# A one-core decoder layer: four places for v tiles on their way out, squares behind the splits, and gate rows turned by TensorE

## Chip, cores and metric

The kernel runs on one core of a Trainium2 chip. The metric is the device time of one execution in microseconds (us), the median over runs. All arithmetic is float32: each operand of a product is split into a rounded high part and a low remainder, and every product is made of three TensorE passes (high by high, high by low, low by high).

## The reference, cut to what matters

```
mod = silu(c) @ w_ada + b_ada;  shift, scale, gate = split(mod, 3)
h = rmsnorm(x, g) * (1 + scale) + shift                      # x is 512 tokens by 2048
q_lat, kv_lat, k_rope, z_mla, u, v, z_sgu, g_mla, g_sgu = split(h @ w_in)
A = causal attention from q_lat, kv_lat, k_rope (16 heads), times silu(z_mla)
v = rmsnorm(v, sgu_norm_g)                                   # a norm over all 2048 columns of v
B = u * (tril(W_s) v_chunk + b_s), times silu(z_sgu)         # 16 groups of 128 columns
merged = sigmoid(g_mla) * A + sigmoid(g_sgu) * B
x = x + gate * (merged @ w_out);  return rmsnorm(x, final_norm_g)
```

Three things of it matter here. The norm of v needs the sum of squares over all columns of v, so the pieces of v are squared as they are made (`ssv`), written out to a DRAM scratch tensor (`v_d`), and read back by group after the norm is known. The gate is a vector over 2048 columns; it is computed with the columns on the partitions (`gate`, 128 by 16), and is needed along the free dimension for all partitions (`grow`). So it goes through a DRAM scratch tensor, `gate_row` (16 by 128), and comes back as a broadcast. And `sigmoid(g_mla) * silu(z_mla)` of head 14 is built from a z that was made early and stored (`z_d`).

## The kernel before, in words

The kernel streams all weights once. A weight granule (128 by up to 1024 numbers) is loaded by SyncE's queue (SP) into one of a few raw places, split by ScalarE (ACT, the high part: a cast) and VectorE (DVE, the low part: a subtraction) into one of two or three places for split weights, and used by TensorE (PE). The program is one list in order for each engine: nothing is reordered at run time, so an instruction that waits holds back everything behind it on its engine. SP is held in the same way: a load waits there until its raw place is free, and stores behind it wait too.

The stages around the change:

**Projection steps, `st` 0 to 25** (`for st, (cg, i) in enumerate(steps)`, L580). Columns of v in three groups `cg` of 384, 384 and 320 columns, eight steps each, and two steps for z. `get` splits the next granule, issues loads, and then runs one, two or three of the pending functions in `pend` (the number is `run`). After a group's last step four `evac_v` (L524), one for each block of 128 tokens, come due: each squares a PSUM bank into a tile (`ssv` gets the sum), copies the bank over it, and hands it to `store`. All of them, and `evac_z`, take their tile from the two places `sig`; `stores` issues a store at the end of the step after the one that made it. Two places for split weights (`w0`, `w1`) alternate, so that the split for the next step can start when the step before has ended.

**v steps, V to -1** (28 of them, V = -28; L1364 and on). The first 1024 columns of v, by seven products in place of eight (sums and differences of blocks). Twelve products a step. `early` and `on(step, phase, ...)` hold what else is done in a step; the phases run in the order FIRST, EVAC, GATE, SPLIT, BACK, then the products, then MISC and LOAD. `v_split` for step s+2 is in phase SPLIT of step s. `v_c12`, `v_c22`, `v_c11`, `v_c21` (L893 to L914) join the pieces of v; `v_done` squares a piece on ScalarE and puts its store into the next step. They run in EVAC, ahead of SPLIT, of the steps V+18, V+20, V+27 and 0.

**Slots 0 and on** (`for s, (p, k) in enumerate(order)`). 24 products of 256 columns each for two of the five other projections; again the split for slot s+2 is in phase SPLIT of slot s, with three places for split weights (`w0`, `w2`, `w1` in turn). `place` puts small VectorE work into slots with room. In slots 0 to 2 stand the end of v and the gate of head 14: `gate_op("z", 14, ..., 0)` (a sigmoid in slot 0, its product in slot 1), `v_norm` in slot 1 (the reduction of `ssv`, a square root on ScalarE, a reciprocal), and `gate_out(0, 4)` in slot 2. The first use of the norm, `sgu_scale`, is in slot 4. `v_load` reads a group of v for it.

```
on(0, EVAC, v_c21, 0)
on(1, EVAC, v_norm)
on(2, LOAD, gate_out, 0, NG)
```

`gate_out` writes four columns of `gate` straight to four rows of `gate_row`: each partition gives four single numbers, `DMA.dma_start(gate_row[a:b].rearrange("j p -> p j"), gate[:, a:b])`.

**Output steps** (L1731 and on). `out_granule(cg, i, ...)` is one granule of 1024 numbers a row of `w_out`, 24 products of 512 columns; step `8*cg + i - 3` runs from 0 (cg 0, i 3) to 20 (cg 2, i 7), and then the last group `cg` 3 runs block by block from weights kept split. In group 2 each step splits two granules, one of group 2 and one of group 3 (`dh`, `dl`), of which the weights stay. In the same steps the last twelve chunks of `w_ada` (1 MB each) are loaded and multiplied with `cact` (`chunk_sum`, twelve sums in the steps 2 to 14); after each fourth chunk (in the steps 5, 10 and 14) `gate_out` follows one step later and `grow_load` two steps later. `residual` (DVE, ACT) multiplies a finished bank with `grow` and adds x, one in each of the first four steps after a group.

Of the kernel before, what the change touches and what calls it, by code (L numbers as in the profile page):

```python
# [11 lines left out]
F32 = mybir.dt.float32  # L12
# [3 lines left out]
AF = mybir.ActivationFunctionType  # L16
# [4 lines left out]
P = 128  # L21
D = 2048
S = 512
# [6 lines left out]
GW = 1024  # L30
# [11 lines left out]
NG = 4  # L42
# [78 lines left out]
def trunk_layer(ctx, tc, xT, xn, c, vecs, pos, wada, w1, w2, wv, wv3, wv4, wh, wh15, wq, wqr, wk, wvv, wo, wsT, bsp, gfin, out,  # L121
                dbg=None):
    nc = tc.nc
    ACT, DVE, PE, DMA = nc.scalar, nc.vector, nc.tensor, nc.sync
# [36 lines left out]
    def nt(p, shape, dt, tag, **kw):  # L161
        uid[0] += 1
        return p.tile(shape, dt, tag=tag, name=f"{tag}_{uid[0]}", **kw)
# [10 lines left out]
    latp = Scope("lat", side=RIGHT)  # L174
# [112 lines left out]
    def get(i, ahead=1, run=1):  # L287
        r = ws.get(i, ahead)
        fs, pend[:] = pend[:run], pend[run:]
        for f in fs:  # L290
            f()
        return r
# [8 lines left out]
    def bank_at(k):  # L301
        return nt(psp.p, [P, S], F32, f"ps{k}")

    def bank():
        n_bank[0] += 1
        return bank_at(ring[(n_bank[0] - 1) % len(ring)])
# [217 lines left out]
    def evac_v(n, cg, ps):  # L524
        m = VW[cg] // P
        w, c0 = m * P, VC[cg]
        t = nt(tb.p, [P, S], F32, "sig", bufs=2)
        ACT.activation(t[:, :w], ps[:, :w], AF.Square, accum_out=ssv[:, n, cg:cg + 1])
        ACT.copy(t[:, :VW[cg]], ps[:, :VW[cg]])
        store(v_d[n][:, c0:c0 + w], t[:, :w])  # L530
        if cg == 2:
            store(kr_d[n], t[:, w:VW[cg]])
# [45 lines left out]
    assert (n_bank[0] - 1) % 8 == 3  # L578
    psv = {}
    for st, (cg, i) in enumerate(steps):  # L580
        wH, wL = get(gb[st], ahead=0 if st == len(steps) - 1 else 1, run={0: 3, 9: 2, 10: 2}.get(st, 1))
        if KC + st < len(DOTS):
            fix_to(FIXED[KC + st], lambda: dot_to(DOTS[KC + st]))
        if cg == "z":
            for k in range(8):
                j = 8 * i + k
                sl = slice(k * P, (k + 1) * P)
                mm3(plain, wH[:, sl], wL[:, sl], hh[j], hl[j], j == 0, j == KC - 1)
            if i == 1:
                pend.append(evac_z)  # L590
        else:
            w = VW[cg]
            if i == 0:
                psv[cg] = [bank_at(k)[:, :w] for k in v_banks[cg]]
            for k in range(2):
                j = 2 * i + k
                sl = slice(k * w, (k + 1) * w)
                for n in range(NB):
                    tk = slice(n * P, (n + 1) * P)
                    mm3(psv[cg][n], hh[j][:, tk], hl[j][:, tk], wH[:, sl], wL[:, sl], j == 0, j == KC - 1)  # L600
            if i == 7:
                for n in range(NB):
                    pend.append(lambda n=n, cg=cg, ps=psv[cg][n]: evac_v(n, cg, ps))
        if 7 <= st < 7 + NG:
            ada_dot(2 * KC + st - 7)
        if st == 8:
            xp.close()
            s12 = Scope("s12")
            for n in ("s1h", "s1l", "s2h", "s2l"):
                sums[n] = nt(s12.p, [P, 8, 256], F32R, n)  # L610
            tb = Scope("tB")
        if st == 6 + NG:
            ada.close()
            c1[0] = Scope("c1", side=RIGHT)
            for n in ("s4h", "s4l"):
                sums[n] = nt(c1[0].p, [P, 8, 256], F32R, n)
        for f in early.pop(st, ()):
            f()
        stores()
# [3 lines left out]
        cols = slice(a, b)  # L623
        tt(gate[:, cols], dots[:, 2 * KC + a:2 * KC + b], vec[:, C_BADA + 2 * KC + a:C_BADA + 2 * KC + b], ALU.add)

    def gate_out(a, b):
        DMA.dma_start(gate_row[a:b].rearrange("j p -> p j"), gate[:, a:b])

    def v_norm():
        gate_sum(0, NG)  # L630
# [9 lines left out]
    def slot(name, dt=F32):  # L640
        return nt(latp.p, [P, S], dt, name)
# [3 lines left out]
    def sig():  # L645
        n_sig[0] += 1
        return slot(f"lat{4 + n_sig[0] % 2}")
# [4 lines left out]
    def on(s, phase, f, *a):  # L652
        assert s >= done[0], (s, done)
        events.setdefault(s, {}).setdefault(phase, []).append(lambda: f(*a))
# [140 lines left out]
    def finish(k, which, s):  # L795

        ty, h = PAIRS[k]["ab".index(which)]
        gate_op(ty, h, res[k, which], s)
# [28 lines left out]
    def evacuate(p, k, s):  # L827

        ps = bank_for(p, k)
        if p == 1:  # L830
            res[k, "a"] = slot(f"lat{k % 2}")
            ACT.copy(res[k, "a"][:, left], ps)
        elif p == 6:
            res[k, "b"] = slot(f"lat{2 + k % 2}")
            ACT.copy(res[k, "b"][:, right], ps)
        elif p == 2:
            ACT.copy(res[k, "b"][:, left], ps)
        elif p == 5:
            t = res[k, "a"][:, left]
            tt(t, ps, t, ALU.add)  # L840
        elif p == 3:
            t = res[k, "b"][:, right]
            tt(t, t, ps, ALU.subtract)
        elif p == 4:
            ACT.copy(res[k, "a"][:, right], ps)
        if (p == 7 and slot_of[k][2] < slot_of[k][7]) or (p == 2 and slot_of[k][7] < slot_of[k][2]):
            def c12():
                t = res[k, "b"][:, left]
                tt(t, bank_for(7, k), t, ALU.subtract)
            if p == 7:  # L850
                c12()
            else:
                on(s + 1, FIRST, c12)
        if p == max((3, 7), key=lambda q: slot_of[k][q]):
            finish(k, "b", s + 1)
        if p == max((4, 5), key=lambda q: slot_of[k][q]):
            finish(k, "a", s + 1)

# [24 lines left out]
            v7[name, t] = slot(tags[t]) if tags[t][:3] == "lat" else nt(tb.p, [P, S], F32, tags[t])  # L883
            ACT.copy(v7[name, t], v7[ps][t])

    def v_done(s, n, part, c0, t, src=None):

        ACT.activation(slot("lat12") if src is None else t, src or t, AF.Square, accum_out=ssv[:, n, part:part + 1])
        if src is not None:
            ACT.copy(t, src)  # L890
        on(s + 1, LOAD, lambda: DMA.dma_start(v_d[n][:, c0:c0 + 512], t))

    def v_c12(s):  # L893
        for t in range(2):
            o = v7["u2", t]
            tt(o, v7["z"][t], o, ALU.subtract)
            v_done(s, t, 3, 512, o)

    def v_c22(s):
        for t in range(2):  # L900
            o = v7["z6", t]
            tt(o, o, v7["y"][t], ALU.subtract)
            v_done(s, 2 + t, 3, 512, o)

    def v_c11(s):
        for t in range(2):
            o = v7["p1", t]
            tt(o, v7["w"][t], o, ALU.add)
            v_done(s, t, 4, 0, o)

    def v_c21(s):
        for t in range(2):
            v_done(s, 2 + t, 4, 0, slot(("lat7", "lat9")[t]), v7["y"][t])

    on(V + 7, EVAC, v_copy, "p1", "y", ("lat11", "lat4"))
    on(V + 8, EVAC, v_copy, "z6", "z", ("lat5", "lat6"))
# [1 line left out]
    on(V + 18, EVAC, v_c12, V + 18)  # L918
    on(V + 20, EVAC, v_c22, V + 20)
    on(V + 27, EVAC, v_c11, V + 27)  # L920
    on(0, EVAC, v_c21, 0)
    on(1, EVAC, v_norm)
    on(2, LOAD, gate_out, 0, NG)
    for s in (18, 20, 27):
        spend(V + s, 1.38)

# [59 lines left out]
    for p in (7, 0, 1, 2, 3, 4, 5, 6):  # L986
        s_ = max(s_, 2 if p in (0, 7) else base[1 + 5 * p + 1])
        on(s_ - 3, LOAD, sgu_load, p)
        on(max(e_ + 1, s_ - 3), LOAD, bias_load, p)
        on(s_ - 3, LOAD, v_load, 2 * p)  # L990
        s_ = place(place(s_, 0.42, sgu_weights), 0.42, sgu_weights_split)
        for q in range(2):
            g = 2 * p + q
            on(s_ + 1, BACK, sgu_scale)
            s_ = place(s_ + 2, 0.69, sgu_split)
            if q == 0:
                on(s_, LOAD, v_load, g + 1)
            s_ += 2
            on(s_, MISC, sgu_mix, q)
            e_ = max(s_, e_) + 1  # L1000
            for half in range(2):
                for part in range(2):
                    e_ = place(e_, 0.48, sgu_out, g, half, part, ("cosT", "sinT")[q] if p == 7 else f"lat{8 + q}")
        sgu_end[p] = e_
        s_ += 4
# [6 lines left out]

    for q in range(2):
        on(base[n_pairs - 2] + 9, LOAD, reload, "t", 14 + q, f"lat{8 + q}")


    acc = []
# [375 lines left out]
    stores()  # L1393
    ws.next_raw, ws.next_part = 2, 1
    done[0] = 0
    gate_op("z", 14, gate_src[0], 0)
    ring[:], n_bank[0] = [bank_of(6), bank_of(7), bank_of(0)], 0
    for s, (p, k) in enumerate(order):
        done[0] = s
# [283 lines left out]
    def grow_load(cg):  # L1683
        cols = slice(cg * S, (cg + 1) * S)
        DMA.dma_start(grow[:, cols], bass.AP(tensor=gate_row.tensor, offset=gate_row.offset + cg * S, ap=[[0, P], [1, S]]))
# [13 lines left out]
    for j, st in chunk_at.items():  # L1699
        later.setdefault(st, []).append(lambda j=j: chunk_sum(j))  # L1700
        later.setdefault(st if j + 2 < KC else 99, []).append(lambda j=j: chunk_load(j + 2))
        if j % 4 == 3:
            later.setdefault(st + 1, []).append(lambda j=j: gate_out(j - 3, j + 1))
            later.setdefault(st + 2, []).append(lambda j=j: grow_load(j // 4))
    later.pop(99)
    for j in (NG, NG + 1):
        chunk_load(j)

# [137 lines left out]
```

## Time and profile before

| | us |
|---|---|
| median of 3 runs (lowest to highest) | 1633.18 (1632.32 to 1635.44) |
| the profiled execution, its own time | 1628.35 |
| its span | 1626.6 |
| TensorE busy in the span | 1594.7 |
| VectorE busy | 1197.8 |
| ScalarE busy | 770.2 |
| mean granted TensorE clock | 0.992 |

The profile is one execution, read from the start of its span. A line of a timeline has the start, the duration, engine, source line, operation and `output<-input`, and in square brackets how long the engine had been idle before and what it waited for. A row of stretches has the stretch, its length, the busy time of PE, of its weight loads (PEld), of DVE, ACT and POOL with the number of instructions, then the granted clock, the share of DMA time, and GB/s. All through, a product counts as busy while it is under way, so a TensorE that runs at a lower clock is as busy as before.

### The profile page before, as it was taken

The numbers are of one execution on the slowest core, as the hardware profiler recorded it, in microseconds if no ns is written. First come the engines' busy times: TensorE is split into PE (matmuls) and PEld (weight loads), VectorE is DVE, ScalarE is ACT, GpSimd is POOL, SyncE is SP. The second block draws the span as 40 slices with busy tenths as digits, with TensorE's granted clock in tenths as the row PEclk, the third lists the DMA queues.
The fourth block names the chain that finished last, engine by engine and source line by source line (L and its number), as shares of the span: only waits on it lengthen the run. The fifth ranks groups of instructions, "written<-read, shape, count | busy, mean of one in ns | idle before, by whom it ended". The sixth has DMA issues, their size and how long they took to land.

```text
span 1626.6 us, 27010 instructions
## 1 busy us (share of the span) xinstructions
PE 1594.7 (98%) x10711; PEld 1484.2 (91%) x10711; DVE 1197.8 (74%) x1751; ACT 770.2 (47%) x1273; POOL 107.9 (7%) x132
## 2 busy tenths in 40 slices
PE   9999999999999999999999999999999999999897
PEld 7888998789999999999999999999889888888676
DVE  8989877758777777777777777667788788857743
ACT  4443335555545454454555555555554555532222
POOL 0000000001111111111111111111000000000000
PEclk9999999999999999999999999999999999999899
DMA  9977556678888897898887989777332222259822
GB/s 379 347 298 297 200 170 202 168 215 203 239 240 252 239 256 204 237 250 208 237 240 197 266 232 248 192 190 198 126 104 88 93 93 87 95 220 322 229 83 104
DMA packets 126865, 335.43 MB, mean 206 GB/s; under 512 B 16393, under 2 KB 37905, under 8 KB 119953
## 3 DMA queue, kind: packets, MB, share of 16 engines
q1 hardware_dynamic: 108290, 273.40, 48.4%
q0 software_dynamic: 18448, 60.30, 21.1%
q8 instruction: 84, 1.38, 0.3%
q14 instruction: 43, 0.35, 0.1%
HBM read 309.45 MB, written 24.20 MB: 205 GB/s over the span
## 4 chain that ended last, share of the span: by engine, by line
PE 83%; DMA 7%; DVE 5%; ACT 2%; issue 2%; SPq 0%; DVEq 0%; ACTq 0%
PE ps L1409 15%; PE ps L1411 15%; PE ps L1410 14%; PE ps L141 11%; PE ps L142 11%; PE ps L140 11%; DMA wada<-in_wada 1%; PE ps L1571 1%; DMA wraw<-in_wo 1%; PE ps L1390 1%; PE ps L1389 1%; PE ps L1388 1%; DVE wada L131 1%; DMA wraw<-in_wh 1%; DMA gate_row<-gate 1%
## 5 line engine op out<-in xcount | busy, mean ns | idle before, releaser
L1409 PE MATMUL ps<-hh,w0h 128*128 128x256 f32 x416 | 118.5, 285 | 0.9 <-DVE lat L128 0.9
L1411 PE MATMUL ps<-hh,w0l 128*128 128x256 f32 x416 | 117.7, 283 | 0.0
L1410 PE MATMUL ps<-hl,w0h 128*128 128x256 f32 x416 | 117.7, 283 | 0.0
L131 DVE SCALAR_TENSOR_TENSOR wada<-wada,cact 128x2048 f32<-128x2048 f32 x47 | 107.2, 2283 | 12.0 <-DMA wada<-in_wada 12.0
L1409 PE MATMUL ps<-hh,w2h 128*128 128x256 f32 x400 | 113.5, 284 | 0.0
L1409 PE MATMUL ps<-hh,w1h 128*128 128x256 f32 x400 | 113.4, 283 | 0.0
L1411 PE MATMUL ps<-hh,w2l 128*128 128x256 f32 x400 | 113.2, 283 | 0.0
L1410 PE MATMUL ps<-hl,w1h 128*128 128x256 f32 x400 | 113.2, 283 | 0.0
L1410 PE MATMUL ps<-hl,w2h 128*128 128x256 f32 x400 | 113.2, 283 | 0.0
L1411 PE MATMUL ps<-hh,w1l 128*128 128x256 f32 x400 | 113.2, 283 | 0.0
L128 DVE TENSOR_TENSOR w2l<-raw,w2h 128x1024 fp32r<-128x1024 f32 x62 | 75.9, 1224 | 44.7 <-ACT w2h L726 39.0
L110 ACT CAST w1h<-wraw 128x1024 fp32r<-128x1024 f32 (+3 forms) x65 | 54.6, 841 | 100.5 <-PE ps L142 40.3
L110 ACT CAST w0h<-wraw 128x1024 fp32r<-128x1024 f32 (+3 forms) x66 | 60.4, 915 | 78.4 <-issue 26.4
L111 DVE TENSOR_TENSOR w0l<-wraw,w0h 128x1024 fp32r<-128x1024 f32 (+3 forms) x66 | 69.2, 1048 | 34.2 <-ACT w0h L110 33.9
L140 PE MATMUL ps<-hh,w1h 128*128 128x512 f32 x226 | 89.8, 398 | 0.2 <-ACT hh L397 0.2
L141 PE MATMUL ps<-hl,w1h 128*128 128x512 f32 x226 | 88.3, 391 | 0.8 <-DVE hl L131 0.8
L706 POOL DMA_DIRECT2D wraw<-in_wh x67 | 59.3, 935 | 441.7 <-DVE w0l L128 206.2
L142 PE MATMUL ps<-hh,w1l 128*128 128x512 f32 x226 | 88.1, 390 | 0.0
L111 DVE TENSOR_TENSOR w1l<-wraw,w1h 128x1024 fp32r<-128x1024 f32 (+3 forms) x65 | 62.5, 962 | 34.0 <-ACT w1h L110 33.0
L128 DVE TENSOR_TENSOR w1l<-wraw,w1h 128x1024 fp32r<-128x1024 f32 x46 | 56.3, 1224 | 41.9 <-ACT w1h L726 37.9
L128 DVE TENSOR_TENSOR w0l<-raw,w0h 128x1024 fp32r<-128x1024 f32 x52 | 63.6, 1223 | 31.9 <-ACT w0h L726 23.9
L128 DVE TENSOR_TENSOR w0l<-wraw,w0h 128x1024 fp32r<-128x1024 f32 x46 | 56.3, 1224 | 38.9 <-ACT w0h L726 37.1
(445 smaller groups left out, 5572.1 us busy)
## 6 DMA issues: line engine op xcount, KB each, us to landing
raw<-in_wh SPq DMA_DIRECT2D x105, 512.0 KB, 6.7
wada<-in_wada SPq DMA_DIRECT2D x47, 1024.0 KB, 7.6
wraw<-in_wh POOLq DMA_DIRECT2D x67, 512.0 KB, 6.8
wraw<-in_wh SPq DMA_DIRECT2D x45, 512.0 KB, 8.2
raw<-in_wh POOLq DMA_DIRECT2D x42, 512.0 KB, 8.4
wraw<-in_wo SPq DMA_DIRECT2D x32, 512.0 KB, 5.1
half<-in_w SPq DMA_DIRECT2D x35, 256.0 KB, 5.1
raw<-in_wv SPq DMA_DIRECT2D x17, 512.0 KB, 5.1
```

What stands on the lines that cost most here:

```text
L110: self.nc.scalar.copy(hi[:, :n], raw[:, :n])
L111: self.nc.vector.tensor_tensor(out=lo[:, :n], in0=raw[:, :n], in1=hi[:, :n].bitcast(F32), op=ALU.subtract)
L128: DVE.tensor_tensor(out=out, in0=in0, in1=in1, op=op)
L131: DVE.scalar_tensor_tensor(out=out, in0=in0, scalar=scalar, in1=in1, op0=op0, op1=op1, **kw)
L140: PE.matmul(ps, ah, bh, start=start, stop=False)
L141: PE.matmul(ps, ah, bl, start=False, stop=False)
L142: PE.matmul(ps, al, bh, start=False, stop=stop)
L706: q_.dma_start(t, wh[h, n, q // 10 - 1], **eng)
L1388: PE.matmul(ps[t], xh[:, tk], wH[:, sl], start=st, stop=False, skip_group_check=True)
L1409: PE.matmul(ps, wH[:, sl], xh, start=st, stop=False, skip_group_check=True)
L1410: PE.matmul(ps, wH[:, sl], xl, start=False, stop=False, skip_group_check=True)
L1411: PE.matmul(ps, wL[:, sl], xh, start=False, stop=sp, skip_group_check=True)
```

## The change

- `evac_v` has four places: token blocks 0 and 1 keep the two `sig` places; blocks 2 and 3 of group 0 take `raw4` and `raw5` of the `c1` pool, of groups 1 and 2 the places of `lat10`, `lat11` and `lat6`. In `get` one pending function a step is run, but three at step 0 (before: two at steps 9 and 10 as well).
- The squares of the pieces of v leave EVAC: `v_done` puts them into BACK, behind the split, one or two steps later, one a step; the store goes to LOAD of that same step. `v_c21` is two parts, in BACK of slots 0 and 1.
- `v_norm` moves from EVAC of slot 1 to FIRST of slot 4, the sigmoid of z of head 14 from slot 0 to slot 5 (its product to 6), the product of u of head 14 from slot 10 to 12. `sgu_scale` stays at slot 4 or later.
- `gate_out` is gone. `gate_turn` transposes four columns of `gate` by PE into a PSUM bank, copies four rows of 128 numbers by DVE, and those go to `gate_row` by one DMA with whole rows. For the first four columns this is in MISC of slot 10, and for the others in the output steps 9, 11 and 17, with the DMA one step and `grow_load` two steps later.

```diff
     def evac_v(n, cg, ps):
...
-        t = nt(tb.p, [P, S], F32, "sig", bufs=2)
+        if n < 2:
+            t = nt(tb.p, [P, S], F32, "sig", bufs=2)
+        elif cg == 0:
+            t = nt(c1[0].p, [P, GW], F32, f"raw{2 + n}")
+        else:
+            t = nt(latp.p, [P, S], F32, "lat10" if n == 2 else "lat11" if cg == 1 else "lat6")
...
-        wH, wL = get(gb[st], ahead=0 if st == len(steps) - 1 else 1, run={0: 3, 9: 2, 10: 2}.get(st, 1))
+        wH, wL = get(gb[st], ahead=0 if st == len(steps) - 1 else 1, run=3 if st == 0 else 1)
...
-    def gate_out(a, b):
-        DMA.dma_start(gate_row[a:b].rearrange("j p -> p j"), gate[:, a:b])
+    def gate_turn(a, b, pg, row):
+
+        PE.transpose(pg[:b - a, :P], gate[:, a:b], ident)
+        DVE.tensor_copy(row[:b - a, :P], pg[:b - a, :P])
+        return lambda: DMA.dma_start(gate_row[a:b], row[:b - a, :P])
...
-            finish(k, "b", s + 1)
+            finish(k, "b", s + 1 + 2 * (k == 0))
...
-    def v_done(s, n, part, c0, t, src=None):
-
-        ACT.activation(slot("lat12") if src is None else t, src or t, AF.Square, accum_out=ssv[:, n, part:part + 1])
-        if src is not None:
-            ACT.copy(t, src)
-        on(s + 1, LOAD, lambda: DMA.dma_start(v_d[n][:, c0:c0 + 512], t))
+    def v_done(s, n, part, c0, t):
+
+        on(s, BACK, lambda: ACT.activation(slot("lat12"), t, AF.Square, accum_out=ssv[:, n, part:part + 1]))
+        on(s, LOAD, lambda: DMA.dma_start(v_d[n][:, c0:c0 + 512], t))
...
-            v_done(s, t, 3, 512, o)
+            v_done(s + 1 + t, t, 3, 512, o)
...
-            v_done(s, 2 + t, 3, 512, o)
+            v_done(s + 1 + t, 2 + t, 3, 512, o)
...
-            v_done(s, t, 4, 0, o)
-
-    def v_c21(s):
-        for t in range(2):
-            v_done(s, 2 + t, 4, 0, slot(("lat7", "lat9")[t]), v7["y"][t])
+            v_done(s + 2 + t, t, 4, 0, o)
+
+    def v_c21(s, t):
+        o = slot(("lat7", "lat9")[t])
+        ACT.copy(o, v7["y"][t])
+        v_done(s + 2, 2 + t, 4, 0, o)
...
-    on(0, EVAC, v_c21, 0)
-    on(1, EVAC, v_norm)
-    on(2, LOAD, gate_out, 0, NG)
+    for t in range(2):
+        on(t, BACK, v_c21, t, t)
+    on(4, FIRST, v_norm)
...
         for q in range(2):
             g = 2 * p + q
+            s_ = max(s_, 3)
             on(s_ + 1, BACK, sgu_scale)
...
+    on(10, MISC, lambda: gate_turn(0, NG, bank(), sig())())
...
-    gate_op("z", 14, gate_src[0], 0)
+    gate_op("z", 14, gate_src[0], 5)
...
-        if j % 4 == 3:
-            later.setdefault(st + 1, []).append(lambda j=j: gate_out(j - 3, j + 1))
-            later.setdefault(st + 2, []).append(lambda j=j: grow_load(j // 4))
     later.pop(99)
+    rows = []
+    for n, (st, k) in enumerate(((9, 0), (11, 1), (17, 4))):
+        a = NG + 4 * n
+        later.setdefault(st, []).append(lambda a=a, k=k: rows.append(
+            gate_turn(a, a + 4, bank_at(k), nt(tp, [P, S], F32, "sig", bufs=3))))
+        later.setdefault(st + 1, []).append(lambda: rows.pop()())
+        later.setdefault(st + 2, []).append(lambda a=a: grow_load(a // 4))
```

## Prediction

> **What bounds the kernel now.** I read the page first, then who TensorE waits for.
>
> ```profile
> span 1626.6 us, 27010 instructions
> PE 1594.7 (98%) x10711; PEld 1484.2 (91%) x10711; DVE 1197.8 (74%) x1751; ACT 770.2 (47%) x1273; POOL 107.9 (7%) x132
> ```
>
> ```profile
> PE ps L140 <- ACT w1h L110: 6.4, 2, 5.2
> PE ps L1409 <- ACT lat L835: 3.0, 1, 3.0
> ```
>
> TensorE is busy for 98% of the span. So only what makes it idle, or lets it run at a lower clock behind an idle stretch, can be won: 31.9 us of idle at most, plus the slow stretches. The idle time has a few places, and in each TensorE waits for a split that ScalarE made late. Next I read ScalarE's timeline there, to see behind what the split stood.
>
> **Place A, the squares of group 0** (projection steps 12 and 13):
>
> ```profile
> 203.57 0.33 PE L140 MATMUL ps<-w1h,hh 128*128 128x384 f32 x1
> 205.03 0.49 ACT L528 ACTIVATE sig<-ps 128x384 f32<-128x384 f32 x1 [4.84 <-DMA v_d<-sig]
> 213.05 0.58 ACT L536 COPY sig<-ps 128x512 f32<-128x512 f32 x1 [5.20 <-DMA v_d<-sig]
> 221.29 0.84 ACT L110 CAST w1h<-wraw 128x768 fp32r<-128x768 f32 x1 [5.58 <-PE ps L142]
> 229.61 0.84 ACT L110 CAST w1h<-wraw 128x768 fp32r<-128x768 f32 x1 [3.28 <-PE ps L142]
> 215.00:220.00 5.00, 4.59 (x17) 4.59 (x18) 4.98 (x10) 0.71 (x1) 0.00 (x0) 0.66 0.74 209
> ```
>
> ScalarE stands 4.84 and 5.20 us for stores out of the two `sig` places, with splits behind it. A step is (229.61 - 221.29)/2 = 4.16 us. Step 11 begins at 203.57, and TensorE frees the next place at 221.2, three steps later: 17.6 against 12.5, so 5.1 us are lost, 1.7 of them in the stretch at clock 0.66. With raw4 and raw5 for blocks 2 and 3 no square waits; a square (0.49, with its accumulator read) and a copy (0.58 or less) fit behind each step's split (0.84) into 4.16. The z copy takes a place whose store has long landed. Taken: 5.1 us, all.
>
> **Places B, C and D** (group 1, group 2, and the first joined pieces of v):
>
> ```profile
> 256.34 0.41 PE L141 MATMUL ps<-w1l,hh 128*128 128x320 f32 x1 [0.45 <-DVE w1l L111]
> 266.85 0.39 PE L1388 MATMUL ps<-w1h,hh 128*128 128x512 f32 x1
> 282.54 0.39 PE L1388 MATMUL ps<-w2h,s1h 128*128 128x512 f32 x1
> 285.26 0.39 PE L1388 MATMUL ps<-w1h,hh 128*128 128x512 f32 x1
> 323.42 0.39 PE L1390 MATMUL ps<-w0l,hh 128*128 128x512 f32 x1
> 325.55 0.50 PE L1390 MATMUL ps<-w2l,hh 128*128 128x512 f32 x1 [0.52 <-DVE w2l L128]
> ```
>
> B: 0.45 us idle, and the product before it drawn out by as much (such a one takes 0.41 at this place), 0.9. C: a v step is 285.26 - 282.54 = 2.72; five of them from 266.85 to 282.54 took 15.69 against 13.60, so 2.1. D: the three products from 323.42 to 325.55 should take 3 x 0.23 and took 2.13: 1.4; there the two squares of `v_c12` stand ahead of the split for the next step. In B and C ScalarE stood for stores from `sig` again. The change takes the cause of each away (lat10, lat11, lat6; squares in BACK). Behind B and C VectorE is next: between 280 and 300 it is nearly full, but the change gives it no more work and it gets back the time in which it idled for ScalarE. Behind D is a load that lands just ahead of the split; I leave 0.2 of it. Taken: 0.9 + 2.1 + 1.4.
>
> **Place E, slots 0 to 13**:
>
> ```profile
> 349.93 1.28 ACT L805 ACT_TABLE_LOAD   x1
> 355.51 0.36 ACT L835 COPY lat<-ps 128x256 f32<-128x256 f32 x1
> 360.40 0.28 PE L1409 MATMUL ps<-hh,w0h 128*128 128x256 f32 x1
> 363.28 0.28 PE L1409 MATMUL ps<-s2h,w2h 128*128 128x256 f32 x1
> 368.02 1.05 ACT L726 CAST w2h<-raw 128x1024 fp32r<-128x1024 f32 x1
> 380.55 1.28 ACT L955 ACTIVATE lat<-lat,rv 128x128 f32<-128x128 f32 x4 [4.62 <-DMA lat<-v_d]
> 352.82:360.40 7.58, 4.63 (x27) 4.47 (x26) 5.74 (x8) 4.07 (x6) 0.00 (x0) 0.77 0.36 102
> 390.98:394.33 3.35, 3.19 (x27) 2.98 (x26) 3.28 (x8) 1.74 (x3) 1.72 (x2) 1.00 0.31 44
> ```
>
> A slot is 363.28 - 360.40 = 2.88. Slot 2 could begin 0.4 us after slot 1 ends (352.82), once ScalarE has copied the bank between them. That copy runs at 355.51, behind four squares, two copies, a sigmoid, a square root and a table load for each of the last two (1.28, the first row). The stretch took 7.58 against 0.4 + 2.88: 4.3 us are won, the slow clock with them, if ScalarE is free at 352.85. By its order after the change it is: one split, one copy and one square stand ahead in slot 1.
>
> What is late next: the same work now stands in slots 1 to 5. Counting ScalarE on from 352.85 with the durations above (split 0.95 back to back, square 0.75, table load 1.30, scale 1.18), with VectorE's addition at slot 4 behind the reciprocal of the norm, I get the split for slot 6 just in time, and in slot 5 the sigmoid with its table load ahead of the split for slot 7 (before: 368.02). Its low part comes 0.75 us late. Queued further behind: the read of the next v group waits for `sgu_split`, and relative to TensorE starts some 2 us later than now; the scale that waits for it (380.55) holds the splits for slots 11 to 13. Before, this chain ended 0.5 us late (the second stretch, 3.35 against 2.88). The flight decides:
>
> ```profile
> lat<-v_d SPq DMA_DIRECT2D x4, 256.0 KB, 8.5
> ```
>
> With the median of 8.5 in place of the 9.5 of this one (the write of `gate_row` with single numbers ran just ahead of it and is gone), and with u's product (0.69 us of VectorE) and one table load out of slots 10 and 11, it ends about 0.9 late, 0.4 worse. Net of E: 4.3 - 0.75 - 0.4 = 3.1. The ends: 4.8 if neither chain is late, and 0 if each is some 2 us late.
>
> The Trainium skill (ScalarE: Activation LUTs, What ACT_TABLE_LOAD costs) gives a switch of tables 1.28 us and a drain of 1.38 more. Here the loads are 1.28, and the one at 349.93 has no idle time before it, so the trace shows no such drain. By the page's figure the two loads in slots 4 and 5 would cost 2.8 more, and the sum would be 23.6.
>
> **Places G and H, the output steps**:
>
> ```profile
> 1509.06 0.43 SPq L627 DMA_DIRECT2D gate_row<-gate  x1
> 1519.81 0.33 SPq L1685 DMA_DIRECT2D gbc<-gate_row  x1
> 1520.71 18.61 SPq L91 DMA_DIRECT2D wraw<-in_wo  x6
> ```
>
> ```profile
> 1464.67 1.05 ACT L110 CAST w1h<-wraw 128x1024 fp32r<-128x1024 f32 x1 [3.12 <-PE ps L142]
> 1470.11 1.06 ACT L110 CAST w0h<-wraw 128x1024 fp32r<-128x1024 f32 x1 [4.38 <-PE ps L142]
> 1502.99 1.05 ACT L110 CAST w0h<-wraw 128x1024 fp32r<-128x1024 f32 x1 [2.39 <-PE ps L142]
> 1529.17 1.04 ACT L110 CAST w1h<-wraw 128x1024 fp32r<-128x1024 f32 x1 [3.73 <-DMA wraw<-in_wo]
> 1572.61 1.05 ACT L110 CAST w0h<-wraw 128x1024 fp32r<-128x1024 f32 x1 [4.38 <-PE ps L142]
> ```
>
> ```profile
> DMA to landing us min/median/max: 4.8/10.2/11.5
> ```
>
> ```profile
> 1486.00:1498.00 12.00, 12.00 (x53) 9.68 (x52) 9.04 (x11) 3.33 (x6) 0.00 (x0) 1.00 0.98 121
> ```
>
> An output step is 1470.11 - 1464.67 = 5.44. From 1502.99 (begin of step 11) to 1572.61 (end of step 20) ten steps took 69.6 against 54.4: 15.2 us lost, idle and slow clock. The 2 KB of `gate_row`, as single numbers, land after a median of 10.2 us (third view, the answer on `gate_row`), and SP stands at the broadcast that reads them (issued only at 1519.81, then the next weights at 1520.71, landed at 1529.1 for a step that was due near 1525). While such a write runs, the DMA engines show a share of 0.98 with 121 GB/s: it also slows the loads beside it. With four whole rows in a DMA of its own, its flight is nearer to that of the other small stores; and the broadcast stands two steps behind the turn, where the row has landed.
>
> What is late next is VectorE:
>
> ```profile
> L131 DVE SCALAR_TENSOR_TENSOR wada<-wada,cact 128x2048 f32<-128x2048 f32 x47 | 107.2, 2283 | 12.0 <-DMA wada<-in_wada 12.0
> ```
>
> ```profile
> 1515.72 1.22 DVE L111 TENSOR_TENSOR w0l<-wraw,w0h 128x1024 fp32r<-128x1024 f32 x1
> 1516.85 0.69 DVE L128 TENSOR_TENSOR sig<-ps,gbc 128x512 f32<-128x512 f32 x1
> 1519.05 0.69 DVE L128 TENSOR_TENSOR y<-y,gfb 128x512 f32<-128x512 f32 x1 [0.79 <-ACT sig L1727]
> ```
>
> In steps 13 and 14 it has two splits (2.4), a residual (2.9 with its wait for the square) and a chunk (2.3): 7.6 in 5.44 us. Step 12 leaves it about 2 us of lead. Stepping its list on with every load in time, the low part for step 16 comes 0.65 us late and all the others 0 to 0.5 early; rounded up for small jitters, 1.0 us stays of the 15.2. Taken: 14.2. The ends: 15.2, and 7 if VectorE or a load is 2 us later in each of four steps.
>
> **New work.**
>
> ```profile
> L1571 PE MATMUL ps<-ident,lat 128*128 128x128 f32 x112 | 16.8, 273 | 0.1
> ```
>
> Four transposes are on TensorE's path: between nothing and 0.273 each; I take 0.1, so 0.4. Each waits for its sum of the gate and holds TensorE while it does. At step 9 that sum is four steps old, at 17 three; at step 11 it is fresh: chunk 11 ends at 1507.35 now, with step 11 ending near 1508.4, and earlier when its load no longer lands behind `gate_row`. VectorE's small copy (below the 0.42 of its quarter-size rows) waits for TensorE, but so does the split behind it. The rows' DMA stands in SP behind a chunk's load, not ahead of a weight that is due. Moving the square root and sigmoid costs nothing beyond E, for their readers come later.
>
> **The sum.** 5.1 + 0.9 + 2.1 + 1.4 + 3.1 + 14.2 - 0.4 = 26.4 us. The profiled execution took 1628.35, so 1601.9; the median of the runs, 1633.18, is 4.8 above it, and from there it is 1606.8. I predict 1607 for the median.
>
> **Rivals.**
> 1. VectorE becomes the bound of the output steps: G and H give 7, not 14.2. For it: 7.6 us of work in two steps of 5.44. Against it: 2 us of lead, and slack in steps 17 to 20. Time 1614.
> 2. ScalarE's jam moves to slots 4 to 13, and E gives 0. For it: two table loads within two slots and the late v read. Against it: three split places give nearly a slot of lead. Time 1610; with rival 1 as well, 1617. The drain of the Trainium skill's page (ScalarE: Activation LUTs, above) would bring most of this rival about; I leave its chance by the trace.
> 3. The new places are not free when asked for (raw4 and raw5 lie where the chunk buffers lay, read by VectorE until about 203.4), or the stores hold ScalarE in another way: A stays. Time 1612. Against it: the square there comes at 204.4.
> 4. Slower: the turn in step 11 stops TensorE, in order, until chunk 11 is summed. It pays each microsecond by which that sum ends after its step. Now it ends 1 us ahead; the 26.4 us are eaten up when it is 27 late, and it is slower by over 0.2% (3.3 us) at 31. For it: chunk loads took up to 12 us here. Against it: the load is asked for two chunk sums earlier, and nothing of that size shows in any row. Time then 1637.
>
> 5. The slow stretch at 215 to 220 is not the child of the gaps before it, and its 1.7 us stay when they go. For it: each gap there was short and products ran between. Against it: the clock falls right behind them, and again behind the 3.0 us of slot 2 (0.77 in the stretch 352.82 to 360.40). Time 1608.5. The Trainium skill speaks for this one (TensorE: Matmul & The Clock Gate, Part 1): there the clock falls only after an idle window of about 3.4 us.
>
> **How the numbers follow.** Forecast 0.57 (1599 to 1611 by the ends of E, of G and H and of the new work, counted from the profiled time below and from the median above), rival 1 0.15, rival 2 0.10, both 0.05, rival 3 0.04, rival 4 0.03, rival 5 0.03, no effect at all 0.03. The range reaches from the forecast's lower end to both first rivals with the 2 us by which the runs spread above their median, 1599 to 1619. 0.2% (3.3 us) is about what a measurement can tell from no change; faster by more has 0.94, within it 0.03, slower 0.03.
>
> **What would show it.** Squares in `evac_v` without waits for `v_d`; no clock below 1.00 near 215; slot 2 beginning 0.4 us behind slot 1; the split for slot 7 and the scale at slot 8 as the new late ones; no stretch above 0.9 DMA share at under 150 GB/s in the output steps; ten output steps in 55 to 56 us. Wrong if those steps still take over 60, or if TensorE waits for a transpose's gate.

## The result, and the profile after

The changed kernel takes 1602.42 us (median of 6 runs, 1601.74 to 1603.01), the kernel before 1633.31 beside it (6 runs, 1629.22 to 1635.44): 0.981 of the time, 95% interval 0.980 to 0.983. The profiled execution of after took 1601.74 (span 1600.0), 26.6 less than the profiled one of before. Between the medians it is 30.9.

The page of after, and who TensorE waits for, with the time in all, the times and the longest:

```profile
span 1600.0 us, 27025 instructions
...
PE 1584.2 (99%) x10715; PEld 1478.6 (92%) x10715; DVE 1197.8 (75%) x1755; ACT 767.7 (48%) x1271; POOL 108.0 (7%) x132
```

```profile
PE ps L1419 <- DVE lat L128: 1.9, 2, 1.1
...
PE ps L141 <- DVE w0l L111: 0.7, 1, 0.7
PE ps L1421 <- DVE w2l L128: 0.6, 1, 0.6
...
PE ps L1419 <- ACT lat L843: 0.5, 1, 0.5
```

TensorE's waits of 6.4 and 3.0 for late splits, and of 3.0 for the late copy of slot 2, are gone. Its idle time is 15.8 us in place of 31.9, and behind the first 20 us no wait is over 1.1. Both kernels issue the same 10,711 products in the same order, besides four transposes in the changed one, so their starts in the two profiled executions can be set side by side. Where the distance grows, time was won:

| place | predicted | found |
|---|---|---|
| start of the kernel (before 20) | 0 | 1.2 |
| A, projection steps 12 and 13 | 5.1 | 5.0 |
| B, group 1 | 0.9 | 1.0 |
| C, first v steps | 2.1 | 2.0 |
| D, step V+18 and on | 1.4 | 1.4 |
| E, slots 0 and on | 3.1 | 1.9 |
| G and H, output steps, less the transposes | 13.8 | 13.7 |
| sum (before rounding) | 26.4 | 26.1 |

The other 0.5 of the 26.6 lies behind the last product. The 1.2 at the start is not the change's: in the second execution of the changed kernel only 0.6 of it was there, and the three parts tried alone below had 0.1 to 0.8. Without it, 24.9 us were found for 26.4.

Place A, ScalarE's timeline and the stretch that was slow:

```profile
202.58 0.84 ACT L110 CAST w0h<-wraw 128x768 fp32r<-128x768 f32 x1 [2.58 <-PE ps L142]
203.32 0.48 ACT L533 ACTIVATE raw<-ps 128x384 f32<-128x384 f32 x1
...
206.74 0.84 ACT L110 CAST w1h<-wraw 128x768 fp32r<-128x768 f32 x1 [2.33 <-PE ps L142]
207.48 0.48 ACT L533 ACTIVATE raw<-ps 128x384 f32<-128x384 f32 x1
```

```profile
215.00:220.00 5.00, 5.00 (x31) 5.00 (x30) 3.19 (x7) 2.18 (x4) 0.00 (x0) 1.00 0.74 236
```

The squares into raw4 and raw5 stand right behind their splits and wait for nothing, the splits follow in 4.16, the clock is 1.00. In place E slot 2 now begins 0.46 us behind slot 1, by TensorE's timeline:

```profile
342.82 0.39 PE L1419 MATMUL ps<-s4h,w1h 128*128 128x256 f32 x1 [0.46 <-ACT lat L843]
```

But two new waits stand. ScalarE's timeline (its first row, the square root of the norm, has no table load ahead of it), VectorE's, and the stretch of the second wait:

```profile
349.94 0.30 ACT L234 ACTIVATE rv<-rv,eps 128x4 f32<-128x4 f32 x1 [0.35 <-DVE rv L639]
...
354.14 1.28 ACT L813 ACT_TABLE_LOAD   x1
355.44 0.63 ACT L813 ACTIVATE lat<-lat 128x512 f32<-128x512 f32 x1
355.98 1.03 ACT L734 CAST w2h<-raw 128x1024 fp32r<-128x1024 f32 x1
```

```profile
357.04 1.23 DVE L128 TENSOR_TENSOR w2l<-raw,w2h 128x1024 fp32r<-128x1024 f32 x1 [3.09 <-ACT w2h L734]
...
365.53 0.41 DVE L128 TENSOR_TENSOR lat<-lat,ps 128x256 f32<-128x256 f32 x1
```

```profile
365.00:370.00 5.00, 3.92 (x34) 3.94 (x34) 4.83 (x9) 2.98 (x7) 0.42 (x1) 1.00 0.37 115
```

The split for slot 7 (355.98) is late behind the table load and the sigmoid, and TensorE idles 0.60 for its low part. VectorE stands 3.09 for the high part, is then busy without a break, and comes late to the sum of 365.53, for which TensorE idles 1.08.

The ten output steps, begin of step 11 to end of step 20, in after (55.79) and before (69.62):

```profile
1490.48:1546.27 55.79, 55.08 (x243) 44.98 (x242) 36.97 (x42) 18.88 (x24) 0.00 (x0) 1.00 0.63 219
```

```profile
1502.79:1572.41 69.62, 60.15 (x241) 47.91 (x240) 38.62 (x40) 19.28 (x24) 0.00 (x0) 0.90 0.69 193
```

### The profile page after: what moved, and what is told of

The parts are those of the page before. It is cut to its first block, busy times and chain, and to the rows that moved or that the text cites. A ratio compares the mean times of both kernels' runs of the same rounds, so it can differ in the third digit from the quotient of the medians.

```text
span 1600.0 us, 27025 instructions
## 1 busy us (share of the span) xinstructions
PE 1584.2 (99%) x10715; PEld 1478.6 (92%) x10715; DVE 1197.8 (75%) x1755; ACT 767.7 (48%) x1271; POOL 108.0 (7%) x132
## 2 busy tenths in 40 slices
DMA packets 124784, 335.42 MB, mean 210 GB/s; under 512 B 14297, under 2 KB 35825, under 8 KB 117873
## 3 DMA queue, kind: packets, MB, share of 16 engines
q8 instruction: 84, 1.38, 0.3%
## 4 chain that ended last, share of the span: by engine, by line
PE 93%; DVE 2%; DMA 2%; ACT 1%; issue 1%; SPq 0%; DVEq 0%; ACTq 0%
PE ps L1419 15%; PE ps L1421 15%; PE ps L1420 15%; PE ps L141 14%; PE ps L142 14%; PE ps L140 13%; PE ps L1400 1%; PE ps L1399 1%; PE ps L1398 1%; PE ps L1581 1%; PE ps L1544 1%; PE ps L1545 1%; DMA wraw<-in_w 1%; DMA rope_d<-half 1%; PE ps L976 1%
## 5 line engine op out<-in xcount | busy, mean ns | idle before, releaser
L128 DVE TENSOR_TENSOR w1l<-raw,w1h 128x1024 fp32r<-128x1024 f32 x52 | 63.6, 1223 | 25.2 <-ACT w1h L734 22.2
```

The costliest lines, as they stand in the source:

```text
L128: DVE.tensor_tensor(out=out, in0=in0, in1=in1, op=op)
```

## The experiments

The edits are cut to what matters; "..." and the comments in them are this text's.

**Each part alone, on the kernel before.** First the rows of the output steps (`rows` and `gate_turn` for the last twelve columns in place of `gate_out`):

```diff
-            later.setdefault(st + 1, []).append(lambda j=j: gate_out(j - 3, j + 1))
-            later.setdefault(st + 2, []).append(lambda j=j: grow_load(j // 4))
+    for n, (st, k) in enumerate(((9, 0), (11, 1), (17, 4))):   # gate_turn, its row, grow_load, as in the change
```

> The kernel before with one part of the change: the gate rows of the output steps turned by TensorE, in the steps 9, 11 and 17. The first four columns still go out as single numbers behind slot 2. Theory (these rows alone carry the gain of the output steps): set side by side product by product, the output steps 11 to 20 took 69.6 us before and 55.8 after the whole change, so this kernel should win 13.8 of the 1628.35 of the profiled execution of before, 1614.5; with runs of before at 1633, a ratio of 0.989 to 0.992. The waits of 5.2, 3.0 and 3.0 us between 200 and 360 stay. Rival (the output steps need the earlier parts too, for instance by the 11 us by which they begin earlier against the weight loads): ten output steps of 60 us or more, ratio 0.994 or above.

Measured: 1615.77, ratio 0.990 (0.988 to 0.991). The stretch of the ten steps:

```profile
1504.05:1559.76 55.71, 55.00 (x243) 44.96 (x242) 36.65 (x42) 18.89 (x24) 0.00 (x0) 1.00 0.64 220
```

55.7, as with the whole change, though they begin 13.6 us later: these rows, in their new places, carry the gain of these steps alone. One thing in the expectation is wrong: the waits of 5.2 us and of one 3.0 did not stand between 200 and 360 but in the output steps, at 1530 and 1554 of the kernel before, and they went. The 3.0 of slot 2 stayed. Second, the places of `evac_v` and its `run`:

```diff
-        t = nt(tb.p, [P, S], F32, "sig", bufs=2)
+        if n < 2: ...   # the four places of the change; run=3 at step 0, else 1
```

> The kernel before with one part of the change: four places for the pieces of v in the projection steps, and one pending function a step. Theory: the stalls of projection steps 12 and 13, of group 1 and of the first v steps go, 5.0 + 1.0 + 2.0 = 8.0 us by the comparison product by product; 1620.3 against the profiled 1628.35, ratio 0.994 to 0.996; the granted clock is 1.00 from 200 to 260. Rival (the clock falls there for another reason than the gaps): a clock well below 1.00 near 215 with no gap ahead of it, and 1.7 us less gain. Rival 3 of the prediction (stores still hold ScalarE): squares with waits of 2 us and more for v_d, gain of 3 us or less.

Measured: 1624.96, ratio 0.995 (0.994 to 0.997); 7.9 us won product by product in A, B and C, and a clock of 1.00 at 215. The ratio is as expected; the time is 4.7 us above the expected 1620.3, which was counted from the profiled execution of before (on this see the point on the median in the account below). Third, squares, norm, sigmoid and the first four columns:

```diff
-    on(0, EVAC, v_c21, 0)
-    on(1, EVAC, v_norm)
+        on(t, BACK, v_c21, t, t)
+    on(4, FIRST, v_norm)     # and v_done in BACK, gate_op at 5, gate_turn in slot 10
```

> The kernel before with one part of the change: squares of the joined pieces behind the splits, norm and sigmoid some slots later, and the first four columns of the gate turned by TensorE in slot 10; the projection steps and the output steps are as before. Theory: 1.4 us in the v steps and 1.9 in the slots (4.0 won at slot 2, 0.8 given back by the split for slot 7, 1.3 given back two slots later by a sum of VectorE that stands behind work delayed by the same sigmoid): 3.3 us, 1625.0 against the profiled 1628.35, ratio 0.997 to 0.999. The two new waits of about 0.6 and 1.1 us stand in the same slots. Rival (the two new waits come from the projection part's earlier start, not from the sigmoid in slot 5): neither wait appears, gain 5 us or more.

Measured: 1629.21, ratio 0.997 (0.996 to 0.998). It won 1.5 in D and 4.0 at slot 2, and lost 0.86 and 1.31 in the same two slots as the changed kernel. So both waits belong to this part. The time is 4.2 us above the expected 1625.0, again with the ratio as expected. The three ratios multiplied give 0.982, the whole change 0.981 (0.980 to 0.983): within the interval the parts add.

**Form or place of the write.** Single numbers, at the steps of the change:

```diff
-        later.setdefault(st + 1, []).append(lambda: rows.pop()())
+        later.setdefault(st + 1, []).append(lambda a=a: gate_out(a, a + 4))   # no gate_turn
```

> The kernel after, with the twelve gate columns of the output steps written as single numbers again, but in the steps in which the changed kernel writes its rows (10, 12 and 18, broadcast one step later); no transposes there. It tells the form of the write from its place in the order. Theory (the form: single numbers fly for some 10 us and slow the loads beside them): SyncE stands at each broadcast, the stretches at a DMA share above 0.9 with less than 150 GB/s come back, output steps 11 to 20 take 65 to 70 us, time 1611 to 1616. Rival (the place: with the last write moved from step 15 to 18, a weight load is no longer queued behind a broadcast at a bad time): these ten steps take 55 to 58 us, time 1602 to 1605.

Measured: 1612.78, ratio 0.988 (0.986 to 0.990); the ten steps took 64.96. The same stretch, first of this kernel, then of after:

```profile
1495.00:1505.00 10.00, 10.00 (x45) 8.26 (x44) 6.02 (x7) 3.05 (x3) 0.00 (x0) 1.00 1.03 126
```

```profile
1495.00:1505.00 10.00, 10.00 (x46) 8.16 (x45) 7.31 (x10) 3.05 (x3) 0.00 (x0) 1.00 0.99 363
```

At the same share of DMA time, 126 GB/s in place of 363. It is the form: 9.2 of the 13.7 come back with it. But of the two stalls that the kernel before has in these steps (TensorE waits 5.2 at 1530 and 3.0 at 1554, each with more behind it) only the first comes back, as 7.2. Behind the last write, in step 18 in place of 15, TensorE waits for nothing, though that write is of single numbers too. For this one the rival is right: the later place was enough. To part SyncE's stand from the slower transfers, the broadcasts were moved away from the writes:

```diff
-    for n, st in enumerate((9, 11, 17)):                                 # broadcast in st + 2
+    for n, (st, ld) in enumerate(((9, 12), (11, 15), (17, 20))):         # broadcast in ld
```

> The changed kernel with the twelve gate columns of the output steps written as single numbers (in the steps 10, 12 and 18, as in the run on the form of the write), but each broadcast two or three steps behind its write (12, 15 and 20 in place of 11, 13 and 19). It parts the two costs of that write: SyncE standing at the broadcast with weight loads behind it, and the slower loads while the write runs. There the ten steps 11 to 20 took 65.0 us. Theory (SyncE's stand is most of it: it stood from 1504.9 to 1517.9 with one short issue): 57 to 59 us, time 1604 to 1606. Rival (the slower loads are most of it: 173 and 78 GB/s in the stretches of the first write): 62 us and more, time 1609 or above.

Measured: 1614.82, ratio 0.988 (0.987 to 0.989), ten steps 67.4: the rival's side. Two issues of SyncE, and from the timelines of VectorE and ScalarE one wait each:

```profile
1503.46 0.33 SPq L1698 DMA_DIRECT2D gbc<-gate_row  x1
1503.83 0.67 SPq L632 DMA_DIRECT2D gate_row<-gate  x1
```

```profile
1517.16 0.69 DVE L128 TENSOR_TENSOR sig<-ps,gbc 128x512 f32<-128x512 f32 x1 [10.92 <-DMA gbc<-gate_row]
```

```profile
1520.89 1.04 ACT L110 CAST w1h<-wraw 128x1024 fp32r<-128x1024 f32 x1 [0.62 <-DMA wraw<-in_wo]
```

The broadcast was issued at once, but beside the next write of single numbers it landed 13.7 us later, and VectorE stood 10.9 for it with the splits behind. In the run before this one (single numbers, broadcast one step later) SyncE and ScalarE show:

```profile
1503.71 1.05 SPq L632 DMA_DIRECT2D gate_row<-gate  x1
1504.86 1.04 SPq L91 DMA_DIRECT2D wraw<-in_wo  x2
1517.89 0.33 SPq L1698 DMA_DIRECT2D gbc<-gate_row  x1
```

```profile
1518.50 1.04 ACT L110 CAST w1h<-wraw 128x1024 fp32r<-128x1024 f32 x1 [6.34 <-DMA wraw<-in_wo]
```

The weight that ScalarE waits for was issued by 1505.9, before SyncE stood for the broadcast, and landed at 1518.4, beside the write of 1503.71. TensorE's longest wait there, 7.2 us, is for this split; the one of 8.2 us in the run with late broadcasts ends with a weight that was issued by 1505.9 too and landed at 1520.8, and ScalarE, held behind VectorE, was ready for it only 0.6 us earlier. So in both the longest wait goes back to slow transfers. What SyncE's stand alone costs wasn't isolated: with late broadcasts one of these also moved into the way of a write.

**What is left: the changed kernel again, and six attempts on its waits.** None of the ratios against before can separate these kernels, so their medians and waits are compared.

> The changed kernel itself once more, as the yardstick for the three beside it. Theory: 1602.4 again, with the same three waits of TensorE in the same places (split for slot 7, a sum of VectorE two slots later, the low part for output step 16), for the order of the work sets them and not chance. Rival (they come from how the transfers fell in that execution): other waits, or the same ones by other amounts, by 0.5 us and more.

Measured: 1602.47, with the same waits; that of output step 16 was 1.0 idle in place of 0.7 (1.3 with drawn out products, in place of 1.0).

```diff
-        gate_src.append(slot("lat3"))
+        gate_src.append(slot("lat8"))
-    gate_op("z", 14, gate_src[0], 5)
+    gate_op("z", 14, gate_src[0], 9)
-    on(4, FIRST, v_norm)
+    on(4, BACK, v_norm)
```

> The changed kernel, with the sigmoid of z of head 14 in slot 9 in place of slot 5 (its z held in another place until then) and the norm of v behind the split of slot 4 in place of ahead of it. Theory: the sigmoid and its table load, 1.9 us of ScalarE ahead of the split for slot 7, make both the wait for that split (0.85 by the comparison product by product) and, through the 3.1 us for which VectorE idles behind it and the backlog after, the wait of two slots later (1.3): both go, 2.2 us, 1600.2. Rival (the second wait is VectorE's own work in these slots, the small rope instructions): only the first goes, 0.8 us, 1601.6. Second rival (the table load is late wherever it stands): the waits turn up around slots 10 and 11, no gain.

Measured: 1603.45. It did not decide: behind the low part the square root ran only at 354.56, the scale and the split for slot 7 after it (356.55), and the two waits shrank by 0.5 and 0.6 alone; product by product 0.9 and 0.7 were lost again near 380 and 416. With the norm left in its place:

```diff
-    gate_op("z", 14, gate_src[0], 5)
+    gate_op("z", 14, gate_src[0], 8)     # z in lat8
```

> The changed kernel with the sigmoid of z of head 14 in slot 8 in place of slot 5, and the norm left ahead of slot 4 (in the kernel of the round before, the norm behind the split held the scale, and so the split for slot 7, just as long: that run did not decide). In slot 8 ScalarE has 2.9 us of waiting for v_d just behind. Theory: the table load and sigmoid (1.9 us) in slot 5 make both waits, 0.85 and 1.3: both go, 2.2 us, 1600.3. Rival (the second wait is the work of VectorE itself, 14 small rope instructions, 3.7 us, in the two slots ahead of the late sum): only the first goes, the second stays at 0.9 or more, 1601.6. Second rival (the work is only moved: the read of v is waited for longer and the splits for slots 11 to 13 come later): 1602 or more.

Measured: 1601.68 (1601.05 to 1602.40). Two stretches of it:

```profile
365.00:370.00 5.00, 5.00 (x44) 5.00 (x43) 2.86 (x5) 3.67 (x8) 0.00 (x0) 1.00 0.52 168
...
410.00:415.00 5.00, 4.09 (x32) 3.68 (x31) 2.26 (x4) 4.93 (x7) 0.78 (x1) 1.00 0.70 240
```

Both waits went, 0.85 and 1.31, so the sigmoid in slot 5 made both. But 1.1 came back from 412 to 414, where in after TensorE idles 0.06. There a scale waits for a read of v, and the splits stand behind it. ScalarE in this kernel, then in after:

```profile
408.51 1.28 ACT L962 ACTIVATE lat<-lat,rv 128x128 f32<-128x128 f32 x4 [3.64 <-DMA lat<-v_d]
```

```profile
409.15 1.28 ACT L962 ACTIVATE lat<-lat,rv 128x128 f32<-128x128 f32 x4 [3.37 <-DMA lat<-v_d]
```

The products are 1.8 us ahead of after, the read only 0.6: the read, not the products, sets the time of that chain.

```diff
+        if cg == 1:
+            pend.append(lambda: None)      # group 1's residuals in steps 14 to 17
```

> The changed kernel, with the four residuals of group 1 one output step later (14 to 17 in place of 13 to 16). Theory (VectorE has 7.6 us of work in each of the steps 13 and 14, 4.3 us too much together, and 2 us of lead): with the residual out of step 13 only step 14 is too full, by 2.2, and the wait in step 16 (1.0 us with the products drawn out beside it) goes or falls below 0.3: 1601.4 to 1601.6. Rival (the low part for step 16 is late because a weight load or the chunk sum is): the wait stays in step 16 or moves to 15, no gain.

Measured: 1602.76; the wait in step 16 is still there, 1.3 us idle where the two executions of the changed kernel have 0.7 and 1.0. VectorE's timeline:

```profile
1510.96 1.23 DVE L111 TENSOR_TENSOR w1l<-wraw,w1h 128x1024 fp32r<-128x1024 f32 x1 [3.37 <-ACT w1h L110]
...
1514.91 2.28 DVE L131 SCALAR_TENSOR_TENSOR wada<-wada,cact 128x2048 f32<-128x2048 f32 x1
...
1518.46 1.22 DVE L111 TENSOR_TENSOR w0l<-wraw,w0h 128x1024 fp32r<-128x1024 f32 x1
```

The time won in step 13 is spent standing for a weight that lands at 1509.9; the residual and the sum of step 14 then still stand ahead of step 16's low part.

> The changed kernel with both of these edits. Theory: the gains add, 3.1 us, 1599.3. Rival (the parts work on the same lead of VectorE or on the same transfers): less than 2 us, 1600.4 or more.

Measured: 1602.75; no gain, as its parts had none.

```diff
-    chunk_at = dict(zip(range(NG, KC), (2, 3, 4, 5, 6, 8, 9, 10, 11, 12, 13, 14)))
+    chunk_at = dict(zip(range(NG, KC), (1, 2, 3, 4, 5, 6, 8, 9, 10, 11, 12, 13)))
```

> The changed kernel with the twelve chunk sums in the output steps 1 to 6 and 8 to 13 in place of 2 to 6 and 8 to 14. The run with the residuals one step later did not shorten the wait of step 16: there VectorE idled 3.4 us for a weight that landed at 1509.9, and then had one split too many ahead of the one for step 16. Theory (what binds is the transfers: from 1485 to 1505 they run at 362 to 383 GB/s, for five chunks and seven granules, while at 1480 to 1485 there are only 116 GB/s): with each chunk one step earlier the weights land earlier, the last sum is out of step 14, and the wait in step 16 (1.0) goes: 1601.4. Rival (the transfers are as full from 1435 to 1470, at 415 to 424 GB/s): sums and splits of steps 1 to 6 come late instead, and it is 1602.4 or slower.

Measured: 1604.01. The wait of step 16 is gone (ten steps in 54.7), as the theory said, but 2.5 us are lost at the beginnings of the steps 5 to 8, most of it in 6 and 7, as its rival said:

```profile
1460.00:1465.00 5.00, 4.30 (x20) 3.25 (x19) 4.06 (x5) 0.00 (x0) 0.00 (x0) 1.00 1.01 418
...
1470.00:1475.00 5.00, 4.58 (x20) 3.49 (x19) 4.18 (x5) 1.67 (x3) 0.00 (x0) 1.00 1.02 419
```

There the transfers run at 418 GB/s; VectorE waits 3.9 and 2.8 us for two chunks (sums at 1454.7 and 1460.9), and the splits and residuals behind these sums come late.

> The changed kernel with the last two edits together. Theory: the gains add, 1599.2. Rival: either edit only moves its wait, 1601 or more.

Measured: 1602.88, the rival's side. The best version is the changed kernel with the sigmoid in slot 8, by 0.7 to 0.8 us between medians whose ranges overlap; it is no safe gain.

## Why the prediction was right, and where it was not

- **A, B, C, D** came as predicted, each within 0.1, and so did their cause: no square of `evac_v` waits for a store. Rival 3 is out. (For D the prediction leaves 0.2 of its 1.4 and then adds up all 1.4; 1.4 came.)
- **Rival 5 (the slow clock has a cause of its own)** is out: with the gaps gone the clock is 1.00, in the changed kernel and with the places alone; where the gaps stay, it falls again (below).
- **E is the term that was mis-sized**: 3.1 against 1.9. Slot 2 gave 4.0 for 4.3 and slot 7 took 0.85 for 0.75. The chain behind the read of v was to end 0.4 worse and ended 0.4 better: the read flew 6.9 us, not 8.5. Two things were missed. The square root needed no table load: with the sigmoid moved behind it, the last load before it is the one at 100.1, for another square root. So there is one load in slots 4 and 5 and not two. And the late split for slot 7 was followed on TensorE alone; on VectorE it left 3.1 us idle, a backlog, and a second wait of 1.3. A last 0.3 is lost around 414. This is rival 2 in part. The drain of 1.38 us that the Trainium skill (ScalarE: Activation LUTs, What ACT_TABLE_LOAD costs) adds to a load does not show: at 354.14 the sigmoid starts 1.30 after its load.
- **G and H** came to 13.7 for 13.8, the one stall in step 16 as foretold, 1.0 us for 0.65. Its cause was named too simply. VectorE is full there, but taking a residual out of step 13 does not help; taking the chunk sum out of step 14 does, at the price of full transfers elsewhere. Rival 1 is out. And not all of it is the form of the write: 9.2 came back with single numbers, but for the last write the later step was enough. Each turn in the output steps costs 0.16 to 0.22 with the step behind it (5.47 and 5.57 for 5.44), not 0.1; the turn of slot 10 costs the predicted 0.1. No turn waits for its sum of the gate: rival 4 is out. The 10.2 us that the prediction reads for the landing of a write is the median of writes and broadcasts together; the three writes of before whose landing the trace has took 10.2 to 11.5, so the argument stands.
- **The way from the profiled execution to the median failed**, by 4.4 us. The 4.8 by which the runs of before stand above their profiled execution were carried over to after, where they are 0.7. In two more executions with the old output steps, those ten took 72.0 and 73.2 in place of 69.6, and where the write of the first four columns stood in its old place the slots took 0.9 and 1.6 more. And at 1628.35 the profiled execution of before is faster than every one of its 37 other runs beside these kernels (1629.22 and above). So it was a cheap one in just the places that the change clears; the changed kernel ends the spread with the cost (its six runs lie within 1.3 us, those of before within 6.2). That this makes up the whole 4.8 is likely by these numbers, but the unprofiled runs cannot be opened.
- **What was luck.** 26.1 us were found for 26.4, but 1.2 of them are the start of the kernel, which the change doesn't touch. And the result lies in the forecast's own range only because its lower end was counted from the profiled time and the upper one from the median. That upper end, 1611, also holds E at 0 and the turns at their dearest, but not G and H at 7, as its words say; with it the sum gives some 1618.

The ten old output steps of the kernel with squares and norm alone, one of the two executions named above:

```profile
1501.66:1574.87 73.21, 62.27 (x242) 48.81 (x241) 38.54 (x40) 19.15 (x24) 0.00 (x0) 0.91 0.71 186
```

## What to carry to other kernels

A write of single numbers costs by what flies beside it, not by its 2 KB: look for stretches where the DMA share is full and the rate is not, and turn the data so that whole rows go out, or move the write: in step 15 TensorE waited 3.0 us and more behind it, in step 18 not at all. A split that is late on one engine is late for whatever the next engine has queued behind it; follow it there before pricing it. Where all runs of a kernel stand above its profiled execution, ask whether that one was a cheap one: here the surplus likely lay in waits that differ from run to run, and it went when the change removed them.

## What was not expected of the hardware

The granted clock falls behind several short gaps. The kernel before with the rows alone, three stretches around place A:

```profile
205.00:210.00 5.00, 4.17 (x23) 3.59 (x22) 2.62 (x4) 2.28 (x7) 0.00 (x0) 1.00 0.23 65
210.00:215.00 5.00, 3.10 (x18) 2.53 (x16) 2.69 (x7) 2.37 (x5) 0.00 (x0) 0.97 0.66 232
215.00:220.00 5.00, 5.00 (x20) 5.00 (x21) 4.97 (x10) 0.29 (x1) 0.00 (x0) 0.68 0.75 216
```

2.7 us of idle time within 10, in gaps of which none keeps two products over 1.7 us apart, and then 0.68 (within that stretch, 215 to 218 has 0.50). In the kernel before it is 1.95 us of idle time, and 0.66. In after, gaps of 0.5, 0.6 and 1.1, each some 8 or more behind the last, leave it at 1.00. The Trainium skill's rule of one idle window of some 3.4 us (TensorE: Matmul & The Clock Gate, Part 1) would not have it fall; its remark on short gaps between groups of products (A second HAM failure mode) is nearer.

With the rows, packets under 512 B went from 16393 to 14297, and the kernel with the output rows alone, which keeps one old write, has 14821: 524 packets for each write of 512 numbers. The Trainium skill (DMA: Bandwidth & Descriptors, Rules for kernel authors) says that a strided last dimension makes one descriptor of each element, and the count agrees to some 2%.
